# The first projection round in four stages of four row tiles, with groups of two blocks and transfers in a forced order

## The chip, the core and the metric

The kernel runs on one core of one Trainium2 chip. The metric is the device time in microseconds (us) of one execution. Before the change it is 1597.13 us, the median of 3 runs (1596.74 to 1597.31).

## The reference

One layer of a hybrid decoder over 256 tokens with 16 meta tokens ahead of them (272 columns), 2048 wide: a root-mean-square norm, one wide input projection, two mixing branches, an output projection, and a squared-ReLU MLP.

```
h = concat(meta_tokens, x)                       # 272 x 2048
xn = rmsnorm(h, norm_mix_g)
proj = xn @ w_in                                 # 2048 x 13336, split into q, k, v, gates
o_fox = forgetting_attention(...)                # 8 heads
o_gla = gated_linear_attention(...)              # 4 heads
y = sigmoid(gate_fox) * (o_fox @ w_o_fox) + sigmoid(gate_gla) * (o_gla @ w_o_gla)
h = h + y @ w_out
h = h + square(relu(rmsnorm(h, norm_mlp_g) @ w_ff1)) @ w_ff2
return rmsnorm(h, final_norm_g)[:, 16:]
```

The change touches only the first seven column blocks of `proj`, and how their operands reach the core.

## The kernel before, in words

Everything is kept transposed: features lie on the 128 partitions, tokens on the free axis, and the 2048 features are 16 row tiles (`KT`). Weights are cut on the host into blocks of 128 output columns; block c is `w_all[c]`, 128 rows of 16 x 128 values, 1 MB. A weight is split into a rounded part `whi` (a cast on ScalarE) and the rest `wlo` (a subtraction on VectorE), both in the type fp32r; an operand x likewise into `x_hi` and `x_lo`. For each row tile and block TensorE makes one wide product (`whi` by hi and lo tokens, 512 columns) and one narrow product (`wlo` by hi tokens, 256 columns); block 7 of the first round, which also needs the meta tokens, has three products of 272 columns instead.

Nearly all of the kernel works block after block: `weight_half` (L108) loads 8 row tiles of a block (512 KB), casts and subtracts, and `gemm2` or `gemm_all` runs the products. The very first round is different (L257 to L363). Since x itself arrives by row tiles, seven blocks (`NF`) run together, each in its own PSUM bank (L262), and the round goes through the row tiles. It has eight stages of two row tiles. In each, `load_h` (L286) fetches two row tiles of h (275 KB), and `load_stage` (L297) two weight pieces: blocks 1 to 4 (512 KB, `wa`) and blocks 5 to 7 (384 KB, `wb`). In stage 0 the first piece is loaded in two halves (L307, L308), blocks 1 and 2 ahead. Rows of a piece are runs of 1 KB.

The order of the work: for each row tile, ScalarE scales h by the norm's gain into `x_hi` (L324), VectorE makes `x_lo` (L325), GpSimd the meta columns of `x_lo` (L328, L329). Then `cut` casts a weight piece (L280) and subtracts (L281). The products of a stage come at L345 and L350, for block 7 at L347, L348 and L352. `square` (L289) squares four row tiles of h at once on ScalarE and adds them up on VectorE for the norm, after stages 3, 5, 6 and 7. The norm's factor is applied after the products, so nothing in the round waits for it. All loads are issued by SyncE.

Raw weights go through five buffers (`RAW`), hi and lo parts through five each (the pool `wp`), shared with all later blocks: a load waits until the piece five before it has been cast and subtracted, a cast until the products of the piece five before it have run. Stages 0 to 2 are loaded ahead, stage s + 3 at the start of stage s.

The framework plans the order on each engine by a model of its own (`schedule_with_timeline_sim`, L1054), so that an engine's order can differ from that of the program. `tc.issue_after(ins)` forces that what is written inside it comes behind `ins` on that engine. Before the change the planner is bound by it at few places: each h load of stages 3 to 7 behind a weight load, the squares behind a cast, and the constants (L369 to L372) behind the round's last load.

After the round: the seven banks are added up and released (L644 on), a small product for the gates' low-rank part runs (L654, L655), the norm's factor comes (L387), and the next block's product begins.

Of the kernel before, what the change touches and what calls it, by code (L numbers as in the profile page):

```python
# [7 lines left out]
F32 = mybir.dt.float32  # L8
# [3 lines left out]
AF = mybir.ActivationFunctionType  # L12
ALU = mybir.AluOpType
# [3 lines left out]
P = 128  # L17
D = 2048
KT = D // P
NM = 16  # L20
NT = 256
NA = NM + NT
# [9 lines left out]
RAW = 5  # L32
# [33 lines left out]
def trunk(ctx: ExitStack, tc: tile.TileContext, hT, w_small, w_all, consts, w_alpha2, out):  # L66
    nc = tc.nc
    serial = [0]

    def nm(s):  # L70
        serial[0] += 1
        return f"{s}_{serial[0]}"
# [11 lines left out]
    def bank(pool, s):  # L84
        return pool.tile([P, 512], F32, tag="bank", name=nm(s))
# [155 lines left out]
    def take(*shape):  # L241
        n = 1
        for d in shape:
            n *= d
        ap = room[:, at_room[0] : at_room[0] + n]
        at_room[0] += n
        if len(shape) == 2:
            ap = ap.rearrange("p (a b) -> p a b", b=shape[1])
        return ap
# [4 lines left out]
    def gain(i, k):  # L254
        return h[:, k, NA + i : NA + i + 1]
# [1 line left out]

    NF = 7  # L260
    warm = bank(px, "warm")
    first_ps = [bank(pg if c < 3 else px, "ps") for c in range(NF)]  # L262
    sqs = [take(4, NA) for _ in range(2)]
    acc = take(4, NA)
    meta = take(KT, NM)

    def first_weights(c0, n, k0):
        raw = wp.tile([P, HK * P], F32, tag="raw", name=nm("raw"), bufs=RAW)
        hi = wp.tile([P, HK, P], F32R, tag="whi", name=nm("whi"))
        lo = wp.tile([P, HK, P], F32R, tag="wlo", name=nm("wlo"))  # L270
        r, hi, lo = (t[:, 0 : 2 * n * P].rearrange("p (c k m) -> p c k m", k=2, m=P)
                     for t in (raw, hi.rearrange("p k m -> p (k m)"), lo.rearrange("p k m -> p (k m)")))

        def load(c, m):
            return nc.sync.dma_start(r[:, c : c + m], w_all[c0 + c : c0 + c + m, :, k0 * P : (k0 + 2) * P].rearrange(
                "c p (k m) -> p c k m", m=P))

        def cut(c, m, ks=slice(0, 2)):
            cs = slice(c, c + m)
            i = nc.scalar.copy(hi[:, cs, ks], r[:, cs, ks])  # L280
            nc.vector.tensor_tensor(lo[:, cs, ks], r[:, cs, ks], hi[:, cs, ks].bitcast(F32), op=ALU.subtract)  # L281
            return i.ins

        return hi, lo, load, cut

    def load_h(eng, k0, n):  # L286
        eng.dma_start(h[:, k0 : k0 + n, :], hT[:, k0 : k0 + n, :])

    def square(q):  # L289
        sq = acc if q == 0 else sqs[q % 2]  # L290
        nc.scalar.activation(sq, h[:, 4 * q : 4 * q + 4, 0:NA], AF.Square)
        if q:
            nc.vector.tensor_tensor(acc, acc, sq, op=ALU.add)

    stages = {}

    def load_stage(s, part):  # L297
        c0, n = ((0, 4), (4, 3))[part]
        w = first_weights(c0, n, 2 * s)
        stages.setdefault(s, []).append(w)  # L300
        return w[2](0, n) if s else w[2]

    load_a, load_b = load_stage(0, 0), load_stage(0, 1)
    load_h(nc.sync, 0, 2)
    load_a(0, 2)  # L307
    load_a(2, 2)  # L308
    load_b(0, 3)
    for cols in (NT, NT, NT, NT):  # L310
        nc.tensor.matmul(warm[:, 0:cols], ones[:, 0:P], ones[:, 0:cols], start=True, stop=True)
    for s in range(1, 3):
        load_h(nc.sync, 2 * s, 2)
        load_stage(s, 0)
        load_stage(s, 1)
    for s in range(KT // 2):
        if s + 3 < KT // 2:
            with tc.issue_after(load_stage(s + 3, 0).ins):
                load_h(nc.sync, 2 * s + 6, 2)
            last = load_stage(s + 3, 1).ins  # L320
        wa, wb = stages[s]
        for kk in range(2):
            k = 2 * s + kk
            nc.scalar.activation(x_hi[:, k], h[:, k, 0:NA], AF.Identity, scale=gain(0, k))  # L324
            nc.vector.scalar_tensor_tensor(x_lo[:, k, 0:NT], h[:, k, NM:NA], gain(0, k),  # L325
                                           x_hi[:, k, NM:].bitcast(F32), op0=ALU.mult, op1=ALU.subtract)
            xm = meta[:, k, :]
            nc.gpsimd.tensor_tensor(xm, h[:, k, 0:NM], gain(0, k).to_broadcast([P, NM]), op=ALU.mult)  # L328
            nc.gpsimd.tensor_tensor(x_lo[:, k, NT:], xm, x_hi[:, k, 0:NM].bitcast(F32), op=ALU.subtract)  # L329
            if s == 0:  # L330
                wa[3](0, 2, slice(kk, kk + 1))
            elif kk == 0:
                for w, n in ((wa, 4), (wb, 3)):
                    copied = w[3](0, n)
        if s == 0:
            wa[3](2, 2)
            for kk in range(2):
                copied = wb[3](0, 3, slice(kk, kk + 1))
        at = [(w[0][:, c], w[1][:, c]) for w, n in ((wa, 4), (wb, 3)) for c in range(n)]

        def products(c, k, part):
            hi, lo = at[c][0][:, k % 2, :], at[c][1][:, k % 2, :]
            ps, st, sp = first_ps[c], k == 0, k == KT - 1
            if part == 0 and c < NF - 1:
                nc.tensor.matmul(ps, hi, x[:, k], start=st, stop=False)  # L345
            elif part == 0:
                nc.tensor.matmul(ps[:, 0:NA], hi, x_hi[:, k], start=st, stop=False)  # L347
                nc.tensor.matmul(ps[:, X_LO], hi, x_lo[:, k], start=False, stop=sp, skip_group_check=True)  # L348
            elif c < NF - 1:
                nc.tensor.matmul(ps[:, 0:NT], lo, x[:, k, 0], start=False, stop=sp)  # L350
            else:
                nc.tensor.matmul(ps[:, 0:NA], lo, x_hi[:, k], start=False, stop=sp)  # L352

        if s < KT // 2 - 1:
            groups = [range(4), range(4, NF)] if s else [range(2), range(2, 4), range(4, NF)]
            order = [(c, 2 * s + kk, part) for g in groups for kk in range(2) for part in range(2) for c in g]
        else:
            order = [(c, 2 * s + kk, part) for c in range(NF) for kk in range(2) for part in range(2)]  # L360
        for o in order:
            products(*o)
        if s in (3, 5, 6, 7):  # L363
            with tc.issue_after(copied):
                square((3, 5, 6, 7).index(s))
    chunk[0] = NF
    nc.gpsimd.memset(wa2, 0.0)
    with tc.issue_after(last):
# [9 lines left out]
    for i in range(2):  # L378
        w = wp.tile([P, HK, P], F32R, tag="whi", name=nm("whi"))
# [269 lines left out]
    ps = bank(pg, "psa")  # L649
    for k in range(KT):  # L650
        if k == HK:
            norm1()
        w = small[k // HK][:, k % HK, :]
# [172 lines left out]
    for j0 in range(0, KT, 2):  # L826
        gates = ahead if j0 == 0 else [gate() for _ in range(4)]
        w = next_weights()
        for j in range(2):
            t = total(gemm2(w, of, k0=8 * j, nk=8))  # L830
            nc.vector.tensor_tensor(gates[2 * j], gates[2 * j], t, op=ALU.mult)
        for j in range(2):
            t = total(gemm2(next_weights(), og))
# [50 lines left out]
    acc = gat.tile([P, NT], F32, tag="acc", name="acc3", bufs=1)  # L884
    for g in range(NG):
        a = operand(keep, "a", tag="s1")
        held = []
        for f in range(KT):
            ps = gemm2(next_weights(), x2)
# [6 lines left out]
        last = g == NG - 1  # L896
# [98 lines left out]
    sqs = half(0, [none] * NL)  # L995
# [63 lines left out]
```

## Time and profile before

| | |
|---|---|
| median of 3 runs | 1597.13 us (1596.74 to 1597.31) |
| the profiled execution's own time | 1596.71 us |
| its span, from the first to the last instruction | 1595.0 us |
| TensorE busy | 1585.0 us, 99% |
| VectorE, ScalarE, GpSimd busy | 1060.4, 790.8, 125.2 us |
| mean rate of the transfers | 184 GB/s; 323 in the first fortieth of the span |

The profile shows one execution. Engines: PE is TensorE's matmul, PEld its weight load, DVE is VectorE, ACT is ScalarE, POOL is GpSimd, SP is SyncE, which issues transfers; a q behind a name (SPq) stands for an engine's instruction sequencer. Of a matmul the start is measured and the end modelled, so the time of one is read from start to start. In brackets stands how long the engine was idle before an instruction, and what released it. L345 is line 345 of the kernel before.

### The profile page before, as it was taken

To read this page: it belongs to the slowest core of one execution; us is meant where nothing else is said; L and a number is where in the kernel's file an instruction comes from. 1 tells how busy PE (TensorE), PEld (TensorE's weight loads), DVE (VectorE), ACT (ScalarE), POOL (GpSimd) and SP (SyncE) were. 2 spreads that over 40 slices of the span, in tenths; PEclk is the share of its full clock that TensorE was granted. 3 is DMA by queue.
4 is the path that set the end of the run, shared out by engine and by line. 5 is a ranking of instruction groups with operands and counts; after the bars stand their busy time and mean duration, and the time that the engine had idled before them with its cause. 6 is when DMAs were issued, how large, how long until landed. Compare 5 with 4: busy or idle time off the path is not lost.

```text
span 1595.0 us, 25427 instructions
## 1 busy us (share of the span) xinstructions
PE 1585.0 (99%) x9812; PEld 1428.8 (90%) x9812; DVE 1060.4 (66%) x1659; ACT 790.8 (50%) x1271; POOL 125.2 (8%) x213
## 2 busy tenths in 40 slices
PE   9999999999999999999999999999999999999997
PEld 8999999999998888888888888888888888888887
DVE  7897757676655555555777776567655776567655
ACT  6665444454455444444555544444444444444563
POOL 6011000011100000000011000000000000000022
PEclk9999999999999999999999999999999999999999
DMA  9444545454445555555555555555555555555552
GB/s 323 156 164 155 180 157 183 167 188 164 159 167 181 191 186 189 189 191 187 186 195 186 188 193 187 188 191 190 187 190 190 186 189 193 186 188 193 186 183 97
DMA packets 86602, 293.09 MB, mean 184 GB/s; under 512 B 9112, under 2 KB 16800, under 8 KB 86352
## 3 DMA queue, kind: packets, MB, share of 16 engines
q1 hardware_dynamic: 85872, 289.62, 53.8%
q8 instruction: 77, 1.26, 0.3%
q0 software_dynamic: 176, 1.12, 0.2%
q10 hardware_dynamic: 432, 0.72, 0.1%
q14 instruction: 45, 0.37, 0.1%
HBM read 289.32 MB, written 2.11 MB: 183 GB/s over the span
## 4 chain that ended last, share of the span: by engine, by line
PE 99%; DMA 0%; issue 0%; POOL 0%; ACT 0%; DVE 0%; SPq 0%; POOLq 0%; ACTq 0%
PE ps L136 51%; PE ps L137 27%; PE psa L155 5%; PE psa L154 5%; PE psa L153 5%; PE ps L345 1%; PE ps L350 1%; PE ps L928 1%; PE pa L548 1%; PE ps L912 0%; DMA raw<-w_all_dram 0%; PE po L611 0%; POOL o L976 0%; PE po L188 0%; PE ps L348 0%
## 5 line engine op out<-in xcount | busy, mean ns | idle before, releaser
L121 DVE TENSOR_TENSOR wlo<-raw,whi 128x1024 fp32r<-128x1024 f32 x522 | 641.0, 1228 | 452.8 <-ACT whi L120 449.4
L120 ACT CAST whi<-raw 128x1024 fp32r<-128x1024 f32 x522 | 548.1, 1050 | 660.0 <-PE ps L136 493.1
L136 PE MATMUL ps<-x,whi 128*128 128x512 f32 x1952 | 683.8, 393 | 0.0
L137 PE MATMUL ps<-x,wlo 128*128 128x256 f32 x1952 | 548.5, 281 | 0.0
L136 PEld LDWEIGHTS ps<-x,whi 128*128 128x128 f32 x1952 | 366.1, 188 | 80.4
L137 PEld LDWEIGHTS ps<-x,wlo 128*128 128x128 f32 x1952 | 368.3, 189 | 0.1
L136 PE MATMUL ps<-a,whi 128*128 128x512 f32 x960 | 334.3, 392 | 0.0
L137 PE MATMUL ps<-a,wlo 128*128 128x256 f32 x960 | 269.1, 281 | 0.0
L136 PEld LDWEIGHTS ps<-a,whi 128*128 128x128 f32 x960 | 179.8, 188 | 39.9
L137 PEld LDWEIGHTS ps<-a,wlo 128*128 128x128 f32 x960 | 181.1, 189 | 0.3
L153 PE MATMUL psa<-x,whi 128*128 128x272 f32 x624 | 181.2, 290 | 0.0
L155 PE MATMUL psa<-x,whi 128*128 128x272 f32 x624 | 181.1, 290 | 0.0
L154 PE MATMUL psa<-x,wlo 128*128 128x272 f32 x624 | 179.4, 288 | 0.0
L153 PEld LDWEIGHTS psa<-x,whi 128*128 128x128 f32 x624 | 118.1, 189 | 0.4
L154 PEld LDWEIGHTS psa<-x,wlo 128*128 128x128 f32 x624 | 117.4, 188 | 0.0
L155 PEld LDWEIGHTS psa<-x,whi 128*128 128x128 f32 x624 | 117.2, 188 | 0.0
L136 PE MATMUL ps<-og,whi 128*128 128x512 f32 x256 | 89.6, 392 | 0.0
L136 PE MATMUL ps<-y,whi 128*128 128x512 f32 x256 | 89.1, 392 | 0.0
L854 POOL TENSOR_TENSOR acc<-acc,hsq 128x256 f32<-128x256 f32 x26 | 28.5, 1097 | 769.2 <-ACT hsq L853 769.2
L137 PE MATMUL ps<-og,wlo 128*128 128x256 f32 x256 | 71.9, 281 | 0.0
L137 PE MATMUL ps<-y,wlo 128*128 128x256 f32 x256 | 71.8, 281 | 0.0
L171 DVE TENSOR_TENSOR evt<-ps,evb 128x256 f32<-128x256 f32 x158 | 65.9, 418 | 0.5 <-ACT evb L168 0.5
(301 smaller groups left out, 1437.0 us busy)
## 6 DMA issues: line engine op xcount, KB each, us to landing
raw<-w_all_dram SPq DMA_DIRECT2D x537, 512.0 KB, 3.6
raw<-w_all_dram SPq DMA_DIRECT2D x8, 384.0 KB, 6.6
h<-hT_dram SPq DMA_DIRECT2D x8, 275.0 KB, 6.7
negc<-fdram POOLq DMA_DIRECT2D x1, 1088.0 KB, 8.0
out_dram<-o SPq DMA_DIRECT2D x2, 512.0 KB, 2.7
raw<-w_all_dram SPq DMA_DIRECT2D x2, 256.0 KB, 3.9
room<-w_small_dram SPq DMA_DIRECT2D x1, 320.0 KB, 7.4
out_dram<-o ACTq DMA_DIRECT2D x1, 320.0 KB, 3.1
```

Of the source, the lines that this page charges most:

```text
L120: nc.scalar.copy(hi[:, k, :], r)
L121: nc.vector.tensor_tensor(lo[:, k, :], r, hi[:, k, :].bitcast(F32), op=ALU.subtract)
L136: nc.tensor.matmul(ps, hi, x, start=first, stop=False)
L137: nc.tensor.matmul(ps[:, 0:NT], lo, x[:, 0, :], start=False, stop=last)
L153: nc.tensor.matmul(ps[:, 0:NA], hi, x_hi[:, k], start=(k == 0), stop=False)
L154: nc.tensor.matmul(ps[:, 0:NA], lo, x_hi[:, k], start=False, stop=(k == KT - 1))
L155: nc.tensor.matmul(ps[:, X_LO], hi, x_lo[:, k], start=False, stop=(k == KT - 1), skip_group_check=True)
L171: nc.vector.tensor_tensor(t, ps[:, 0:NT], b, op=ALU.add)
L345: nc.tensor.matmul(ps, hi, x[:, k], start=st, stop=False)
L350: nc.tensor.matmul(ps[:, 0:NT], lo, x[:, k, 0], start=False, stop=sp)
L548: nc.tensor.matmul(dst, k[:, a], q[:, a, :], start=(a == 0), stop=(a == 1))
L854: nc.gpsimd.tensor_tensor(acc, acc, sq, op=ALU.add)
```

## The change

The round has four stages (`KS` = 4 row tiles each) of four groups: blocks 1 and 2, 3 and 4, 5 and 6, and 7 alone. Each pair of stage and group is a unit with one weight piece (512 KB, or 256 KB for block 7, in runs of 2 KB); there are 16, as there were 16 pieces. The first unit's piece is loaded block by block, and the first four row tiles of h two by two; later stages load four at once, ahead of their first unit. Each load is forced behind the one before it. Five units are loaded ahead, and unit i + 5 is loaded at unit i. The x tiles of a stage are made before its first unit is cut. The products of a group go row tile by row tile, in the last stage block by block. A stage's square comes after its second unit.

```diff
-    NF = 7
+    NF, KS = 7, 4
+    GROUPS = ((0, 2), (2, 2), (4, 2), (6, 1))
...
-    sqs = [take(4, NA) for _ in range(2)]
-    acc = take(4, NA)
+    sqs = [take(KS, NA) for _ in range(2)]
+    acc = take(KS, NA)
...
     def square(q):
         sq = acc if q == 0 else sqs[q % 2]
-        nc.scalar.activation(sq, h[:, 4 * q : 4 * q + 4, 0:NA], AF.Square)
+        nc.scalar.activation(sq, h[:, KS * q : KS * q + KS, 0:NA], AF.Square)
...
-    def load_stage(s, part):
-        c0, n = ((0, 4), (4, 3))[part]
-        w = first_weights(c0, n, 2 * s)
-        stages.setdefault(s, []).append(w)
-        return w[2](0, n) if s else w[2]
...
-    load_a, load_b = load_stage(0, 0), load_stage(0, 1)
-    load_h(nc.sync, 0, 2)
-    load_a(0, 2)
-    load_a(2, 2)
-    load_b(0, 3)
...
+    units = [(s, c0, n) for s in range(KT // KS) for c0, n in GROUPS]
+    loaded, queue = [], [None]
+
+    def in_turn(load, *args):
+        with tc.issue_after(queue[0]) if queue[0] else nullcontext():
+            queue[0] = load(*args).ins
+
+    def load_unit():
+        i = len(loaded)
+        s, c0, n = units[i]
+        w = first_weights(c0, n, KS * s)
+        loaded.append(w)
+        if i == 0:
+            in_turn(load_h, nc.sync, 0, 2)
+            in_turn(w[2], 0, 1)
+            in_turn(w[2], 1, 1)
+            in_turn(load_h, nc.sync, 2, 2)
+        else:
+            if c0 == 0:
+                in_turn(load_h, nc.sync, KS * s, KS)
+            in_turn(w[2], 0, n)
...
-        if s < KT // 2 - 1:
-            groups = [range(4), range(4, NF)] if s else [range(2), range(2, 4), range(4, NF)]
-            order = [(c, 2 * s + kk, part) for g in groups for kk in range(2) for part in range(2) for c in g]
-        else:
-            order = [(c, 2 * s + kk, part) for c in range(NF) for kk in range(2) for part in range(2)]
+    for _ in range(RAW):
+        load_unit()
+    for i, (s, c0, n) in enumerate(units):
+        w = loaded[i]
+        cs = range(c0, c0 + n)
+        if i == 0:
+
+            for k in range(KS):
+                x_tile(k)
+                if k % 2:
+                    for c in cs:
+                        copied = w[3](c, 1, slice(k - 1, k + 1))
+            order = [(c, k + kk, part) for k in (0, 2) for c in cs for kk in range(2) for part in range(2)]
+        else:
+            if c0 == 0:
+                for k in range(KS * s, KS * s + KS):
+                    x_tile(k)
+            copied = w[3](0, n)
+            if s < KT // KS - 1:
+                order = [(c, KS * s + kk, part) for kk in range(KS) for part in range(2) for c in cs]
             else:
-                nc.tensor.matmul(ps[:, 0:NA], lo, x_hi[:, k], start=False, stop=sp)
...
+                order = [(c, KS * s + kk, part) for c in cs for kk in range(KS) for part in range(2)]
+        if len(loaded) < len(units):
+            load_unit()
         for o in order:
-            products(*o)
-        if s in (3, 5, 6, 7):
+            products(w, c0, *o)
+        if c0 == 2:
             with tc.issue_after(copied):
-                square((3, 5, 6, 7).index(s))
+                square(s)
+    last = queue[0]
```

`first_weights` takes `KS` row tiles per piece instead of 2. `x_tile` and `products` hold the same instructions as before, as functions. The constants are loaded behind the last unit's load.

## Rows read from the trace of the kernel before

**Rows 1.** The page's first section: busy us (share of the span) and instructions by engine.
```profile
PE 1585.0 (99%) x9812; PEld 1428.8 (90%) x9812; DVE 1060.4 (66%) x1659; ACT 790.8 (50%) x1271; POOL 125.2 (8%) x213
```

**Rows 2.** All waits of TensorE: us in total, times, longest.
```profile
PE warm L311 <- DVE ones L195: 1.3, 1, 1.3
PE pn L952 <- ACT sq L933: 0.7, 1, 0.7
PE ps L345 <- ACT whi L280: 0.4, 1, 0.4
```

**Rows 3.** TensorE's timeline, end of the round: start us, us, what.
```profile
40.74 0.39 PE L345 MATMUL ps<-x,whi 128*128 128x512 f32 x1
...
44.91 0.29 PE L347 MATMUL ps<-x,whi 128*128 128x272 f32 x1
...
45.29 0.29 PE L347 MATMUL ps<-x,whi 128*128 128x272 f32 x1
...
45.67 0.29 PE L207 MATMUL prb<-csh,ones 128*128 128x272 f32 x1
...
49.93 0.28 PE L153 MATMUL psa<-x,whi 128*128 128x272 f32 x1
```

**Rows 4.** Timeline of all engines, 0 to 12 us.
```profile
4.55 0.70 ACT L280 CAST whi<-raw 128x256 fp32r<-128x256 f32 x2
...
5.00 0.96 PE L345 MATMUL ps<-x,whi 128*128 128x512 f32 x2
5.08 0.81 DVE L281 TENSOR_TENSOR wlo<-raw,whi 128x256 fp32r<-128x256 f32 x2
...
6.40 0.62 ACT L280 CAST whi<-raw 128x512 fp32r<-128x512 f32 x1 [1.15 <-DMA raw<-w_all_dram]
...
7.51 0.93 ACT L280 CAST whi<-raw 128x384 fp32r<-128x384 f32 x2 [0.49 <-DMA raw<-w_all_dram]
...
8.27 0.90 POOL L328 TENSOR_TENSOR room<-h 128x16 f32<-128x16 f32 x2 [2.65 <-DMA h<-hT_dram]
8.34 0.93 ACT L324 ACTIVATE x<-h 128x272 fp32r<-128x272 f32 x2
...
9.70 1.89 ACT L280 CAST whi<-raw 128x1024 fp32r<-128x1024 f32 x2 [0.43 <-DMA raw<-w_all_dram]
...
11.00 1.54 PE L345 MATMUL ps<-x,whi 128*128 128x512 f32 x6
```

**Rows 5.** TensorE's timeline in short windows: the first products, and the pause.
```profile
5.56 0.40 PE L345 MATMUL ps<-x,whi 128*128 128x512 f32 x1
...
6.26 0.40 PE L345 MATMUL ps<-x,whi 128*128 128x512 f32 x1
...
7.07 0.50 PE L345 MATMUL ps<-x,whi 128*128 128x512 f32 x1 [0.41 <-ACT whi L280]
...
7.40 0.39 PE L345 MATMUL ps<-x,whi 128*128 128x512 f32 x1
7.63 0.54 PE L350 MATMUL ps<-x,wlo 128*128 128x256 f32 x3
```

**Rows 6.** The round as one stretch: us, PE, PEld, DVE, ACT, POOL busy, PEclk, DMA, GB/s.
```profile
5.00:45.67 40.67, 40.26 (x241) 35.72 (x241) 31.61 (x47) 29.15 (x46) 20.87 (x34) 1.00 0.94 310
```

**Rows 7.** Casts and subtractions of 1024 columns in the round: busy us, mean ns.
```profile
L281 DVE TENSOR_TENSOR wlo<-raw,whi 128x1024 fp32r<-128x1024 f32 x7 | 8.6, 1225 | 3.5 <-ACT whi L280 3.5
...
L280 ACT CAST whi<-raw 128x1024 fp32r<-128x1024 f32 x7 | 7.3, 1041 | 2.3 <-DMA raw<-w_all_dram 2.3
```

**Rows 8.** ScalarE's timeline: the first square, and the next block's first cast.
```profile
18.43 1.11 ACT L291 ACTIVATE room<-h 128x1088 f32<-128x1088 f32 x1
...
40.83 1.05 ACT L120 CAST whi<-raw 128x1024 fp32r<-128x1024 f32 x1
```

**Rows 9.** Two stretches early in the round, columns as in rows 6.
```profile
4.00:6.00 2.00, 2.00 (x7) 1.22 (x6) 1.63 (x4) 1.25 (x4) 1.59 (x5) 1.00 0.78 216
7.00:10.00 3.00, 2.93 (x18) 2.66 (x19) 2.53 (x5) 2.08 (x6) 1.71 (x4) 1.00 1.07 373
```

More of the change, by code (lines that the diff above doesn't have):

```diff
@@ L270, in first_weights, with cut @@
         lo = wp.tile([P, HK, P], F32R, tag="wlo", name=nm("wlo"))
-        r, hi, lo = (t[:, 0 : 2 * n * P].rearrange("p (c k m) -> p c k m", k=2, m=P)
+        r, hi, lo = (t[:, 0 : KS * n * P].rearrange("p (c k m) -> p c k m", k=KS, m=P)
                      for t in (raw, hi.rearrange("p k m -> p (k m)"), lo.rearrange("p k m -> p (k m)")))
         def load(c, m):
-            return nc.sync.dma_start(r[:, c : c + m], w_all[c0 + c : c0 + c + m, :, k0 * P : (k0 + 2) * P].rearrange(
+            return nc.sync.dma_start(r[:, c : c + m], w_all[c0 + c : c0 + c + m, :, k0 * P : (k0 + KS) * P].rearrange(
                 "c p (k m) -> p c k m", m=P))
-        def cut(c, m, ks=slice(0, 2)):
+        def cut(c, m, ks=slice(0, KS)):
             cs = slice(c, c + m)
@@ L286, in load_h @@
     def load_h(eng, k0, n):
-        eng.dma_start(h[:, k0 : k0 + n, :], hT[:, k0 : k0 + n, :])
+        return eng.dma_start(h[:, k0 : k0 + n, :], hT[:, k0 : k0 + n, :])
     def square(q):
         sq = acc if q == 0 else sqs[q % 2]
-        nc.scalar.activation(sq, h[:, 4 * q : 4 * q + 4, 0:NA], AF.Square)
+        nc.scalar.activation(sq, h[:, KS * q : KS * q + KS, 0:NA], AF.Square)
         if q:
             nc.vector.tensor_tensor(acc, acc, sq, op=ALU.add)
-    stages = {}
-    def load_stage(s, part):
-        c0, n = ((0, 4), (4, 3))[part]
-        w = first_weights(c0, n, 2 * s)
-        stages.setdefault(s, []).append(w)
-        return w[2](0, n) if s else w[2]
@@ L305, in trunk, with x_tile @@
-    load_a, load_b = load_stage(0, 0), load_stage(0, 1)
-    load_h(nc.sync, 0, 2)
-    load_a(0, 2)
-    load_a(2, 2)
-    load_b(0, 3)
+    def x_tile(k):
+        nc.scalar.activation(x_hi[:, k], h[:, k, 0:NA], AF.Identity, scale=gain(0, k))
+        nc.vector.scalar_tensor_tensor(x_lo[:, k, 0:NT], h[:, k, NM:NA], gain(0, k),
+                                       x_hi[:, k, NM:].bitcast(F32), op0=ALU.mult, op1=ALU.subtract)
+        xm = meta[:, k, :]
+        nc.gpsimd.tensor_tensor(xm, h[:, k, 0:NM], gain(0, k).to_broadcast([P, NM]), op=ALU.mult)
+        nc.gpsimd.tensor_tensor(x_lo[:, k, NT:], xm, x_hi[:, k, 0:NM].bitcast(F32), op=ALU.subtract)
@@ new lines, in products @@
+    def products(w, c0, c, k, part):
+        hi, lo = w[0][:, c - c0, k % KS, :], w[1][:, c - c0, k % KS, :]
+        ps, st, sp = first_ps[c], k == 0, k == KT - 1
+        if part == 0 and c < NF - 1:
+            nc.tensor.matmul(ps, hi, x[:, k], start=st, stop=False)
+        elif part == 0:
+            nc.tensor.matmul(ps[:, 0:NA], hi, x_hi[:, k], start=st, stop=False)
+            nc.tensor.matmul(ps[:, X_LO], hi, x_lo[:, k], start=False, stop=sp, skip_group_check=True)
+        elif c < NF - 1:
+            nc.tensor.matmul(ps[:, 0:NT], lo, x[:, k, 0], start=False, stop=sp)
+        else:
+            nc.tensor.matmul(ps[:, 0:NA], lo, x_hi[:, k], start=False, stop=sp)
@@ L310, in trunk @@
     for cols in (NT, NT, NT, NT):
         nc.tensor.matmul(warm[:, 0:cols], ones[:, 0:P], ones[:, 0:cols], start=True, stop=True)
[L312 to L350, printed above, removed]
-            else:
-                nc.tensor.matmul(ps[:, 0:NA], lo, x_hi[:, k], start=False, stop=sp)
-        if s < KT // 2 - 1:
-            groups = [range(4), range(4, NF)] if s else [range(2), range(2, 4), range(4, NF)]
-            order = [(c, 2 * s + kk, part) for g in groups for kk in range(2) for part in range(2) for c in g]
-        else:
-            order = [(c, 2 * s + kk, part) for c in range(NF) for kk in range(2) for part in range(2)]
@@ new lines, in trunk @@
+    for _ in range(RAW):
[10 more added lines that the diff above has]
+            order = [(c, k + kk, part) for k in (0, 2) for c in cs for kk in range(2) for part in range(2)]
+        else:
+            if c0 == 0:
[4 more added lines that the diff above has]
+                order = [(c, KS * s + kk, part) for kk in range(KS) for part in range(2) for c in cs]
+            else:
+                order = [(c, KS * s + kk, part) for c in cs for kk in range(KS) for part in range(2)]
+        if len(loaded) < len(units):
+            load_unit()
```

## The prediction, made before the change was run

> **What bounds the kernel now.** I read the page's totals first, then TensorE's waits, and only then the first 46 us, where the whole change lies. TensorE is busy for 1585.0 us, 99% of the span [rows 1], and the only waits that it has anywhere are 1.3 us for the ones at the start, 0.7 us at the end and 0.4 us for a cast in the first round [rows 2]. So a transfer, a cast or a subtraction costs time only where TensorE stands for it, and in the first round that can be counted.
>
> Work of the round: with the operands there, twelve pairs of a wide and a narrow product run from 40.74 to 44.91, 0.347 us each, and the three products of block 7 take 0.38 us (44.91 to 45.29) [rows 3]. One row tile is thus 6 x 0.347 + 0.38 = 2.46 us, and 16 of them 39.4 us. The round takes from 5.00 [rows 4] to 45.67 [rows 3], 40.67 us. **1.3 us are lost in it now**: about 0.3 us on the very first product, which took 0.56 us (5.00 to 5.56) instead of 0.23 (7.40 to 7.63), about 0.6 us between the starts at 6.26 and 7.07 [rows 4, 5] (0.23 us would do; the idle time in that row is only 0.41 because it counts from a modelled end), and some 0.4 us in small pieces. From 7.07 on TensorE is full: 40.26 us busy in the 40.67 [rows 6].
>
> So no more than 1.3 us can be won in the round, 0.08% of 1597 us. What a measurement of this kernel can tell from no change is about 0.2%, 3.2 us.
>
> **The change, part by part.** The 240 products, their weight loads and all bytes stay. Seventeen weight transfers stay seventeen; eight of h become five, so SyncE issues 22 instead of 25. Casts become 4 of 256 columns, 11 of 1024 and 4 of 512 instead of 19 of other sizes, over the same columns. These edits cost nothing by themselves, since ScalarE and VectorE work 29.15 and 31.61 of the 40.67 us [rows 6] beside TensorE; without that cover a lengthened cast would cost its full length. What counts is when each operand is there.
>
> Start. The first product needs 275 KB of h, then 256 KB of weights, as now, and comes at 5.00 again, behind one cast of 256 columns [rows 4].
>
> Block 2. Now the next 256 KB carry blocks 3 and 4; after the change they carry block 2, which the first products have without them today. They land at 6.40, where the waiting cast starts. One 256-column cast is 0.35 us (two take 0.70) [rows 4], so block 2 starts at about 6.8. Block 1 has two row tiles by then, 0.69 us of work and the same slow first product, and is done at about 6.05. **Idle 0.75 us.** Block 2's narrow products wait for VectorE's subtraction, 0.4 us (two take 0.81 [rows 4]), half of it hidden; its two row tiles end at 7.7. The bound on the other side, an earlier landing, is rival one.
>
> Row tiles 3 and 4. 275 KB of h took 0.76 us in the queue (7.51 to 8.27 [rows 4]); from 6.4 this makes 7.2. An x tile is 0.47 us on ScalarE (two take 0.93 [rows 4]) and a pass of about 0.4 on VectorE, and in program order the casts for these rows stand behind both x tiles: TensorE goes on at 8.1 (if the planner puts the casts first, their weights having landed) to 8.45. **Idle 0.4 to 0.75 us.** Four pairs, 1.39 us, end at 9.5 to 9.85.
>
> Blocks 3 and 4. 512 KB took 1.43 us (8.27 to 9.70 [rows 4]), so they land at 8.6. One cast of 1024 columns is 1.04 us and its subtraction 1.23 [rows 7]: with ScalarE free at 8.75, the wide products can start at 9.8, the narrow ones at 11.0. If the planner puts all eight wide products first (it does such things: the six wide ones in a row at 11.00 [rows 4] are out of the written order), only 0.3 us is lost; in written order 0.5 us is. **Idle 0.1 to 0.7 us.**
>
> These pieces with the slow first product: 0.33 + 0.75 + 0.2 + 0.4 to 0.75 + 0.1 to 0.7, 1.8 to 2.7 us lost, against 0.9 us in the same stretch now.
>
> Later blocks. Each transfer of 512 KB takes 1.43 us and feeds eight pairs, 2.78 us of TensorE. Blocks 5 and 6 land at 10.0 and block 7 at 10.8, before TensorE asks for them at 12.5 to 13.4. The first square, 1.11 us on ScalarE, now at 18.43 [rows 8], may come between these casts, as it is tied only to the cast of blocks 3 and 4: 0 to 0.4 us. Stage two: h of four row tiles lands at 12.3, weights at 13.7; four x tiles take 1.9 us, cast and subtraction 2.3, so ready at 16.5, with TensorE busy to 16.8 or 17.7. It holds, but narrowly.
>
> SyncE's forced order. A load waits for the raw buffer of five units before, and all later ones, h too, queue behind it. What hides this is five units of look-ahead, five times 2.5 us of TensorE; a load late by more than that would cost the rest. Zero.
>
> End of the round. The next block's first cast waits for a hi buffer of this round: now at 40.83 [rows 8], used at 49.93 [rows 3]. The last stage goes block by block in longer pieces, so that buffer comes free 1 to 2 us later, and the slack is several us: zero. Banks are evicted earlier: zero, as nothing waits for them.
>
> **Sum.** 0.9 to 1.8 us more lost in stage one, 0 to 0.4 for the square, small gaps as now: +0.9 to +2.2 us. I take +1.2, nearer the lower end, because of the planner's reordering in the row just named. The profiled execution is 1596.71 us around a span of 1595.0, and 0.42 below the median; +1.2 makes 1597.9 of it, and of the median of 1597.13 **1598.3 us**. Bounds: -1.3 (all present loss gone) to +2.2.
>
> **A rule against it.** The row first: after its present pause TensorE goes on with 0.33 and then 0.23 us for a wide product [rows 5], at a granted clock of 1.00 before and behind it [rows 9]. The Trainium skill, TensorE: Matmul & The Clock Gate, section Part 1: The HAM clock gate, says that the array's default is half its clock, and that idling gives the full clock back. By that rule the pauses that the change adds could drop it to the lower level, and the time would be that of rival three.
>
> **Rivals.**
> One, the early transfers come faster and the pauses shrink. Between 4 and 6 us only 216 GB/s flowed, between 7 and 10 us 373 [rows 9]; at the later pace the second 256 KB take 0.7 us and would land at 5.2 instead of 6.40, since the first landed before the cast at 4.55 [rows 4]. For it: the runs are 2 KB instead of 1 KB. Against: nothing in the profile says that the run's length made the slow stretch. Then block 2 follows block 1 at once, h comes at 6.0, and the loss is 0.9 to 1.8 us instead of 1.3: -0.4 to +0.5, **1597.2 us**. Chance 24%.
>
> Two, slower by more than 0.2%: the early pace lasts, and stage two starves. At 216 GB/s from 7.2 on, blocks 3 and 4 land at 9.6, 5 and 6 at 12.1, 7 at 13.3, the 550 KB of h at 15.9 and the next weights at 18.3; ready at 20.6 while TensorE ends stage one at 18.3. That is 2.3 us, and 0.9 for the later start, beyond the forecast: **1601.5 us**. It decides from where stage two's first weights land after about 15.5. Against: in that very place the trace has 373 GB/s. Chance 5%.
>
> Three, the clock falls in the pauses. The 4.9 us of work between 7 and 13 us would take 4.9 us more at the 1.2 GHz level than at 2.4: up to **1603 us**. Against: the row above, and pauses of 0.75 us at most. Chance 3%.
>
> Four, the change moves nothing that TensorE sees: the planner fills the pauses with other products, and it stays full from 7 us on: 1597.1 us. Chance 8%.
>
> **Numbers.** Forecast 58%; 24, 5, 3 and 8% for one to four; 2% for what I don't see. The range takes in the lower bound of -1.3 (1595.8) and goes past the upper one of +2.2 (1599.3) by 1.1 us, for a landing of block 2 or of blocks 3 and 4 that late again: 1595.8 to 1600.4. Slower by over 0.2% are two, three and nothing of the forecast's own bounds: 8%. Faster by over 0.2% would need 3.2 us where 1.3 are to be had: 2%. The rest, 90%, is within 0.2%.
>
> **What would show it.** Right: first product at 5.0, a pause of some 0.7 us before block 2 ended by a cast, another before row tile 3 ended by x or a cast, the round's end at 46.5 to 48.0 instead of 45.67, and the same shape from there on. Wrong: a round that ends at 45.2 or before, waits of TensorE after 18 us, a granted clock below 1.00 inside the round, or a difference that arises behind it.

## The result, and the profile after

The kernel after takes **1599.73 us** (median of 22 runs, 1598.89 to 1601.23); beside it, on the same chips, the one before takes 1596.93 us (22 runs, 1596.6 to 1598.25). The ratio is 1.0017, 95% interval 1.0011 to 1.0023: slower by 2.8 us, just inside the 0.2% that count as no change here. The forecast of 1598.3 had the sign; the size is above it, and inside the range. One execution of the second experiment below (1941.52 us), one of the fourth (1721.81) and a few of the kernel before beside them were far longer than the rest; they are left out of the ratios and of what is said on the clock.

The profiled execution of the kernel after took 1599.13 us, 2.4 more than that of the kernel before. First the page's totals, columns as in [rows 1]:

```profile
span 1597.4 us, 25421 instructions
...
PE 1586.0 (99%) x9812; PEld 1428.9 (89%) x9812; DVE 1061.5 (66%) x1659; ACT 791.4 (50%) x1271; POOL 123.2 (8%) x213
```

All engines do nearly what they did [rows 1]; the span is 2.4 us longer. What TensorE waited for, in the view of its waits, columns as in [rows 2]:

```profile
PE warm L341 <- DVE ones L195: 1.3, 1, 1.3
PE ps L331 <- ACT whi L281: 0.9, 2, 0.5
PE pn L958 <- ACT sq L939: 0.7, 1, 0.7
PE ps L336 <- DVE wlo L282: 0.5, 1, 0.5
PE ps L331 <- DVE x L298: 0.2, 1, 0.2
```

The first and the third line were there before. The 0.4 us for a cast [rows 2] have become 0.9 us for two casts, and a subtraction (`wlo`) and an x tile are new. Where they lie is seen in the timeline of all engines, 0 to 13 us (columns as in [rows 4]):

```profile
3.86 0.94 ACT L297 ACTIVATE x<-h 128x272 fp32r<-128x272 f32 x2 [1.77 <-DMA h<-hT_dram]
...
4.96 0.71 ACT L281 CAST whi<-raw 128x256 fp32r<-128x256 f32 x2 [0.16 <-DMA raw<-w_all_dram]
...
5.42 0.80 PE L331 MATMUL ps<-x,whi 128*128 128x512 f32 x1 [0.36 <-ACT whi L281]
...
6.01 0.45 PE L336 MATMUL ps<-x,wlo 128*128 128x256 f32 x1
...
6.25 0.50 PE L331 MATMUL ps<-x,whi 128*128 128x512 f32 x1
...
6.59 0.28 PE L336 MATMUL ps<-x,wlo 128*128 128x256 f32 x1
6.92 0.71 ACT L281 CAST whi<-raw 128x256 fp32r<-128x256 f32 x2 [1.25 <-DMA raw<-w_all_dram]
...
7.37 0.50 PE L331 MATMUL ps<-x,whi 128*128 128x512 f32 x1 [0.50 <-ACT whi L281]
...
8.74 0.50 PE L331 MATMUL ps<-x,whi 128*128 128x512 f32 x1 [0.17 <-DVE x L298]
...
8.98 1.05 ACT L281 CAST whi<-raw 128x1024 fp32r<-128x1024 f32 x1 [0.41 <-DMA raw<-w_all_dram]
...
9.94 1.10 ACT L292 ACTIVATE room<-h 128x1088 f32<-128x1088 f32 x1
10.07 1.23 DVE L282 TENSOR_TENSOR wlo<-raw,whi 128x1024 fp32r<-128x1024 f32 x1 [0.97 <-ACT whi L281]
...
10.24 0.63 PE L331 MATMUL ps<-x,whi 128*128 128x512 f32 x2
...
11.35 0.51 PE L336 MATMUL ps<-x,wlo 128*128 128x256 f32 x2 [0.48 <-DVE wlo L282]
...
13.10 0.63 PE L331 MATMUL ps<-x,whi 128*128 128x512 f32 x2
```

Read it from start to start, at 0.23 us for a wide and 0.12 us for a narrow product. The first product comes at 5.42 instead of 5.00 [rows 4]: its cast stood for the transfer until 4.96. Block 1's four products take 1.29 us (5.42 to 6.71, 0.12 behind the start at 6.59) for 0.69 us of work: **0.6 us lost**. Then TensorE stands until 7.37 for block 2's cast, which stood 1.25 us for its transfer: **0.66**. Between 7.37 and 8.74 lie 1.37 us for 0.69 of work again, **0.68** (some 0.2 of it for block 2's subtraction, the rest before and at row tile 3). At 10.24 two wide products start, end at 10.70, and the narrow ones behind them wait for the subtraction of 1024 columns to 11.35: **0.65**. The next unit follows at 13.10 with no wait. The end of the round, in TensorE's timeline:

```profile
47.69 0.28 PE L338 MATMUL ps<-x,wlo 128*128 128x272 f32 x1
47.81 0.29 PE L660 MATMUL psa<-x,whi 128*128 128x272 f32 x1
...
52.08 0.29 PE L153 MATMUL psa<-x,whi 128*128 128x272 f32 x1
```

The round ends at 47.81 instead of 45.67 [rows 3], 2.14 us later, and the product at L153 comes at 52.08 instead of 49.93 [rows 3]: the same 2.15. It stays so to the last product, which starts at 1589.19 instead of 1587.04. The remaining 0.25 us of the span lie behind that, at the last stores. The round as one stretch, columns as in [rows 6]:

```profile
5.42:47.81 42.39, 41.24 (x240) 35.85 (x241) 32.26 (x48) 29.92 (x47) 17.75 (x34) 1.00 0.84 291
```

Of 42.39 us some 3.0 are lost, against 1.27 before: 1.72 more, and 0.42 for the later start. Hardly anything is lost or won after 12 us.

### The profile page after: what moved, and what is told of

Same layout as the page of the kernel before. It is cut to its first block, busy times and chain, and to the rows that moved or that the text cites. A ratio compares the mean times of both kernels' runs of the same rounds, so it can differ in the third digit from the quotient of the medians.

```text
span 1597.4 us, 25421 instructions
## 1 busy us (share of the span) xinstructions
PE 1586.0 (99%) x9812; PEld 1428.9 (89%) x9812; DVE 1061.5 (66%) x1659; ACT 791.4 (50%) x1271; POOL 123.2 (8%) x213
## 4 chain that ended last, share of the span: by engine, by line
PE 98%; DMA 0%; issue 0%; POOL 0%; DVE 0%; ACT 0%; SPq 0%; POOLq 0%; ACTq 0%
PE ps L136 51%; PE ps L137 27%; PE psa L155 5%; PE psa L154 5%; PE psa L153 5%; PE ps L331 1%; PE ps L336 1%; PE ps L934 1%; PE pa L554 1%; PE ps L918 0%; DMA raw<-w_all_dram 0%; PE po L617 0%; POOL o L982 0%; PE po L188 0%; PE psa L661 0%
## 5 line engine op out<-in xcount | busy, mean ns | idle before, releaser
L153 PE MATMUL psa<-x,whi 128*128 128x272 f32 x624 | 181.2, 290 | 0.0
L153 PEld LDWEIGHTS psa<-x,whi 128*128 128x128 f32 x624 | 118.1, 189 | 0.4
```

The costliest lines, as they stand in the source:

```text
L153: nc.tensor.matmul(ps[:, 0:NA], hi, x_hi[:, k], start=(k == 0), stop=False)
```

## The experiments

Theory A: the loss is work that is not there. With two blocks at a time, the first pieces that land carry half the TensorE work per x tile, so TensorE outruns the transfers, and nothing else matters. Rivals: B, the forced order of the transfers costs it; C, the landing of the first weights is later for their shape (runs of 2 KB); D, the pauses bring TensorE to its lower level. The experiments are counted in the order of their headings; the last is the second of the two kernels under the last heading.

### The forced order taken away

```diff
-        with tc.issue_after(queue[0]) if queue[0] else nullcontext():
-            queue[0] = load(*args).ins
+        queue[0] = load(*args).ins
```

> The changed kernel without the forced order of its loads; the planner then issues the h loads of the second, third and fourth stage earlier, from the ninth load on. Theory A (the whole loss is TensorE waiting for operands in the first 12 us, because two blocks at a time give it half the work per landed x tile): no change, ratio to before 1.0012 to 1.0022, round's end at 47.8 us +-0.3. Rival B (the forced order queues loads behind waits): 1 us or more comes back, ratio under 1.001.

Measured: 1600.16 us (11 runs), ratio 1.0019 (1.0011 to 1.0028), that of the kernel after. Without the force the h loads of the third and fourth stage are issued at 6.32 and 7.87 us instead of 13.66 and 20.59, and nothing comes back of the 1 us or more that B wanted: the forced order costs nothing, and **B falls**. The profiled execution was a long one (1601.14 us), with the round's end at 49.75, which no theory had. TensorE's timeline tells why:

```profile
8.33 0.80 PE L330 MATMUL ps<-x,whi 128*128 128x512 f32 x1 [0.68 <-ACT whi L281]
...
9.17 0.63 PE L330 MATMUL ps<-x,whi 128*128 128x512 f32 x1
...
9.60 0.41 PE L335 MATMUL ps<-x,wlo 128*128 128x256 f32 x1
...
49.75 0.29 PE L659 MATMUL psa<-x,whi 128*128 128x272 f32 x1
```

The wide product at 9.17 takes 0.43 us to the next start, twice 0.23, and so it goes until 13.5 us. In that execution the first weights had landed at 5.49 (4.93 in the kernel after) and block 2's at 7.85 (6.89). The windows of that execution (columns as in [rows 9]) show it from another side:

```profile
9.10:12.40 3.30, 3.30 (x13) 2.75 (x12) 2.13 (x4) 2.88 (x4) 0.95 (x3) 1.00 1.04 412
```

Thirteen products in 3.3 us, TensorE "busy" throughout, where full pace gives nineteen; the granted clock is printed as 1.00 all the same, since the trace's first record of the clock stands only at 13.5 us.

### The first four row tiles as before, the other twelve as after

The round begins with two stages of two row tiles and groups of four and three blocks; from row tile 5 on it has the stages, groups and forced order of the change.

```diff
-    units = [(s, c0, n) for s in range(KT // KS) for c0, n in GROUPS]
+    units = [(k0, 2, c0, n) for k0 in (0, 2) for c0, n in ((0, 4), (4, 3))]
+    units += [(k0, KS, c0, n) for k0 in range(KS, KT, KS) for c0, n in GROUPS]
...
```

> The first four row tiles go as before the change (two stages of two, blocks 1 to 4 and 5 to 7, runs of 1 KB), the other twelve as after it, all loads forced. Theory A: first product at 5.0, one pause of about 0.6 us, round's end at 45.7 us +-0.4, ratio 0.9995 to 1.0005. Rival B: the loss stays, ratio above 1.001. If the rest of the new scheme (groups of two, runs of 2 KB, longer last stage) were worth anything, the round would end before 45.4.

Measured: 1597.32 us (11 runs), ratio 1.0003 (0.9994 to 1.0011). The timeline:

```profile
4.56 0.70 ACT L281 CAST whi<-raw 128x256 fp32r<-128x256 f32 x2
...
5.00 0.73 PE L330 MATMUL ps<-x,whi 128*128 128x512 f32 x2
...
5.81 0.62 ACT L281 CAST whi<-raw 128x512 fp32r<-128x512 f32 x1 [0.56 <-DMA raw<-w_all_dram]
...
45.58 0.29 PE L663 MATMUL psa<-x,whi 128*128 128x272 f32 x1
```

First product at 5.00, end of the round at 45.58 (before 45.67 [rows 3]). Within the interval, **all of the loss comes from the first four row tiles**; the other three quarters of the change, and the forced order once more, cost and bring nothing that shows.

### The first piece by rows: blocks 1 and 2 together, two row tiles of them at a time

```diff
...
-            in_turn(w[2], 0, 1)
-            in_turn(w[2], 1, 1)
+            in_turn(w[2], 0, 2, 0, 2)
             in_turn(load_h, nc.sync, 2, 2)
+            in_turn(w[2], 0, 2, 2, 4)
```

> The changed kernel, but its first weight piece is loaded as rows 1 and 2 of both blocks (runs of 1 KB), then h of row tiles 3 and 4, then rows 3 and 4 of both blocks. Theory A: block 2 follows block 1 without a pause, but the pause before row tile 3 grows, as the same bytes must have landed by then: TensorE goes on there at 8.4 to 8.7 (8.74 after the change), gain 0 to 0.4 us. Rival C (runs of 2 KB made the first landings late by 0.5 us): first weights land at 4.4 instead of 4.9, first product at 5.0, and all that follows comes 0.5 us earlier: gain 0.5 to 0.8 us.

Measured: 1599.15 us (11 runs), ratio 1.0015 (1.0006 to 1.0023). In TensorE's timeline:

```profile
7.71 0.81 PE L331 MATMUL ps<-x,whi 128*128 128x512 f32 x2 [0.95 <-ACT whi L281]
...
47.86 0.29 PE L660 MATMUL psa<-x,whi 128*128 128x272 f32 x1
```

The first product came at 4.95, as C had it, the pause before block 2 was gone, and TensorE was at row tile 3 a whole microsecond earlier (7.71, not 8.74; A had 8.4 to 8.7). In the profiled execution the round ended where it had (47.86): the time was lost again, in three waits for casts and one for a subtraction, because blocks 3 and 4 land no sooner. **A pause moved is not a pause won**, and C's earlier first landing by itself is worth nothing in that execution. The median is 0.6 us below that of the kernel after, which is a gain of the size that C wanted, but the two intervals overlap, and the profile shows no such gain. One of these eleven runs has a mean clock of 0.997, against nine of the 22 of the kernel after; whether that is the difference stays open.

### The pauses filled

The warm-up is half a product longer, and behind block 1's four products five more run into the warm-up's bank, which nothing reads.

```diff
-    for cols in (NT, NT, NT, NT):
+    for cols in (NT, NT, NT, NT, P):
...
+                    for _ in range(5):
+                        with tc.issue_after(mm.ins):
+                            mm = nc.tensor.matmul(warm[:, 0:NT], ones_r[:, 0:P], ones_r[:, 0:NT], start=True, stop=True)
```

> The changed kernel with TensorE kept busy in its first two pauses: one more warm-up product of 128 columns ahead of the first product, and five products of the ones (0.12 us each) between block 1 and block 2, into a bank that nobody reads. Theory A (waiting for operands alone): the same time to +0.2 us, and the same spread between executions. Rival D (part of the loss is TensorE at its lower clock level because of the pauses, in some executions more than in others): the clock is granted in full about 1 us earlier than at 6.46, the mean granted clock of all executions is 0.998 or more, the slower half of the executions disappears, and the median falls by 0.4 to 0.9 us.

Measured: 1599.53 us (12 runs), ratio 1.0017 (1.0008 to 1.0026). TensorE's timeline:

```profile
6.85 0.76 PE L372 MATMUL warm<-ones 128*128 128x256 f32 x5
...
47.58 0.29 PE L673 MATMUL psa<-x,whi 128*128 128x272 f32 x1
```

The round ends 0.23 us sooner, as much as blocks 3 and 4 landed sooner (their cast began at 8.76, not 8.98), and the median falls by 0.2, of the 0.4 to 0.9 that D wanted. Nor did full pace begin earlier, as D had it: the narrow product at 6.29 still took 0.22 us to the next start. The mean granted clock was 0.998 or 0.999 in its runs, where 9 of the 22 of the kernel after have 0.997. So **D is at most a small part** of the median.

### The kernel before, its first stage row tile by row tile

The way opposite to the change: more blocks per x tile, in pieces of one row tile (runs of 512 bytes).

```diff
...
-    load_h(nc.sync, 0, 2)
-    load_a(0, 2)
-    load_a(2, 2)
-    load_b(0, 3)
+    prev = load_h(nc.sync, 0, 1)
+    for ld, args in ((load_a, (0, 2, 0, 1)), (load_a, (2, 2, 0, 1)), (load_h, (nc.sync, 1, 1)),
+                     (load_b, (0, 3, 0, 1)), (load_a, (0, 4, 1, 2)), (load_b, (0, 3, 1, 2))):
...
```

> The kernel before, whose first stage goes row tile by row tile over all seven blocks: h of row tile 1 alone (137 KB), then its weights for blocks 1 and 2, 3 and 4, then h of row tile 2, then the rest (runs of 512 B). Theory A (the start is bound by the bytes that must have landed per us of TensorE's work): 265 KB instead of 531 KB stand before the first product, so it comes 0.3 to 0.8 us earlier than 5.0, and the round ends 0 to 0.8 us before 45.67, at most 0.05% of the time. Rival C (short runs land late): the first weights land no earlier than 4.3, and the round ends at 45.7 or later.

Measured: 1598.09 us (11 runs), ratio 1.0008 (1.0000 to 1.0017). TensorE's timeline:

```profile
4.50 1.35 PE L347 MATMUL ps<-x,whi 128*128 128x512 f32 x4
...
7.11 0.73 PE L347 MATMUL ps<-x,whi 128*128 128x512 f32 x2 [0.79 <-ACT whi L280]
...
46.94 0.29 PE L207 MATMUL prb<-csh,ones 128*128 128x272 f32 x1
```

The start came half a microsecond earlier, as A had it, but the gain was lost and 1.3 us besides: a pause of 0.79 at 7.11 and another of 0.98 at 12.1, since the pieces of the second stage landed at 11.03 instead of 9.68. Against A in its plain form: work per x tile is not all, the arrival of the following pieces counts as much. The first weights (128 KB) were cast from 3.59 on, so short runs did not make them late, as C had it.

### The first block in two halves, in runs of 1 KB

```diff
...
-            in_turn(w[2], 0, 1)
+            in_turn(w[2], 0, 1, 0, 2)
+            in_turn(w[2], 0, 1, 2, 4)
```

> The changed kernel, but its very first weight load (block 1, four row tiles, 256 KB in runs of 2 KB) goes as two loads of 128 KB in runs of 1 KB. If the length of the runs made the first landing late (4.9 to 5.5 us where two blocks in runs of 1 KB landed at 4.3), both halves have landed by 4.4 and the first product comes at 5.0. If it is that one block is read at a time, or anything else, the second half lands at 4.9 or later; the first half, half the bytes, may land before 4.5 either way. The time stays within 0.1% of the changed kernel's in both.

Measured: 1601.72 us (9 runs), ratio 1.0028 (1.0018 to 1.0037). The timeline:

```profile
4.38 0.39 ACT L281 CAST whi<-raw 128x256 fp32r<-128x256 f32 x1
...
5.28 0.40 ACT L281 CAST whi<-raw 128x256 fp32r<-128x256 f32 x1 [0.52 <-DMA raw<-w_all_dram]
...
7.72 0.51 PE L332 MATMUL ps<-x,whi 128*128 128x512 f32 x1 [1.07 <-ACT whi L281]
```

The whole 256 KB of block 1 are there at 5.26, later than in runs of 2 KB (4.93), so C's "2 KB" alone is not the reason. Block 2 starts at 7.72 (7.37 after), and the time grew where no theory had it grow. Its profiled execution (1599.48 us) has a mean clock of 0.999; the other eight have 0.996 or 0.997, and take 1600.18 to 1602.49.

### The kernel before with half of the warm-up

```diff
-    for cols in (NT, NT, NT, NT):
+    for cols in (NT, NT):
```

> The kernel before with two warm-up products instead of four, so that TensorE stands idle from 3.3 to 5.0 us; nothing else changes. Rival D (idle time ahead of the first product holds TensorE at its lower level for longer, and that was part of what the change cost): wide products take 0.43 instead of 0.23 us for 3 us and more after 5.0, the round ends 0.7 to 2 us after 45.67, ratio 1.0004 to 1.0013. Theory A alone: round's end within 0.3 us of 45.67.

Measured: 1597.94 us (11 runs), ratio 1.0006 (0.9997 to 1.0015). TensorE's timeline:

```profile
6.78 1.91 PE L345 MATMUL ps<-x,whi 128*128 128x512 f32 x4
...
47.75 0.29 PE L207 MATMUL prb<-csh,ones 128*128 128x272 f32 x1
```

Here products went at half pace (0.43 us for a wide one, 0.21 for a narrow one) until 11.2 us, and the profiled round ended at 47.75, 2.08 late, of which 0.3 is a later first landing. So **D's mechanism exists**: in this execution TensorE ran at its lower level for some microseconds, with less work ahead of the first product. That less work is what brings it is made likely, not shown, since one execution of the first experiment did the same behind the whole warm-up. The median grew by only 1.0 us, so most executions paid less than the profiled one, which was the longest of its kernel.

### Blocks 3 and 4 cut in two halves

To take the wait at 11.35 away, the cast and the subtraction of 1024 columns go as two of 512.

```diff
-            copied = w[3](0, n)
+            if i == 1:
+                w[3](0, n, slice(0, 2))
+                copied = w[3](0, n, slice(2, 4))
+            else:
+                copied = w[3](0, n)
```

> The changed kernel, but the piece of blocks 3 and 4 in its first stage is cast and subtracted in two halves, row tiles 1 and 2, then 3 and 4. Theory A: the wait of 0.48 us for the subtraction at 11.35 goes, and the products after it come 0.5 to 0.9 us earlier; round's end 0.5 to 0.9 us earlier than it would be at the same landing of the piece (47.81 at a landing of 8.96). If TensorE's pace there were set by something else, the wait stays.

Measured: 1600.09 us (10 runs), ratio 1.0019 (1.0009 to 1.0028). TensorE's waits:

```profile
PE ps L331 <- ACT whi L281: 2.5, 2, 1.9
```

The wait for the subtraction is gone, yet nothing is gained: in the profiled execution the first weights landed at 5.20 and block 2's at 8.27, a pause of 1.88 us. Behind it the windows show the clock fall (columns as in [rows 9]):

```profile
9.10:12.40 3.30, 3.30 (x11) 2.71 (x11) 2.59 (x6) 2.88 (x5) 1.45 (x4) 0.50 1.04 410
12.50:15.00 2.50, 2.50 (x15) 2.17 (x15) 1.50 (x2) 2.50 (x6) 1.20 (x2) 1.00 1.04 381
```

A granted clock of 0.50 (1.2 GHz) and 11 products in 3.3 us, then 1.00 (2.4 GHz) again. What the halved cut is worth by itself stays open, since the landing and the clock covered it.

### What the landing hangs on: two kernels

The first 256 KB of weights landed 0.65 to 0.68 us behind h in the four kernels that load them as two blocks of two row tiles at once (before, the second, the third and the seventh experiment), and 1.09 to 1.85 us behind it where they are one block of four row tiles (after, and the first, fourth and eighth experiment). Two kernels part block and run length: the kernel before with its first piece block by block (1 KB runs), and the kernel after with its first two blocks in one transfer (2 KB runs).

```diff
-    load_a(0, 2)
-    load_a(2, 2)
+    for c in range(4):
+        load_a(c, 1)
```

> The kernel before, whose first 512 KB of weights (blocks 1 to 4, two row tiles) go as four loads of one block each instead of two loads of two blocks; runs of 1 KB as before. From the landing of the first h to that of these 512 KB it took 2.1 to 2.7 us where blocks were read in pairs, 3.0 to 4.8 us in the changed kernel, which reads them one at a time. If reading one block at a time is what makes the landings late: 3.0 us or more here, round's end 0.3 us or more behind 45.67, ratio 1.0002 to 1.001. If it is the run's length or the number of row tiles: 2.1 to 2.7 us, round's end as before.

```diff
-            in_turn(w[2], 0, 1)
-            in_turn(w[2], 1, 1)
+            in_turn(w[2], 0, 2)
```

> The changed kernel, but its first weight piece (blocks 1 and 2, four row tiles, 512 KB, runs of 2 KB) is one load instead of two of one block. If reading one block at a time makes the landings late: the 512 KB land 2.1 to 2.7 us behind the first h, at 5.8 to 6.5 instead of 6.9 to 8.3; the first product comes later (6.2 to 6.9 instead of 5.4), but everything from row tile 3 on comes 0.5 us or more earlier than in the changed kernel, except for what the lower clock level costs after the longer idle time. If it is the length of the runs: 3.0 us or more again, and the time is that of the changed kernel or longer.

Measured: 1597.38 us (10 runs), ratio 1.0002 (0.9992 to 1.0011), and 1599.48 us (11 runs), ratio 1.0017 (1.0008 to 1.0026). The timeline of the first:

```profile
5.05 0.71 ACT L280 CAST whi<-raw 128x256 fp32r<-128x256 f32 x2 [0.41 <-DMA raw<-w_all_dram]
...
6.25 0.62 ACT L280 CAST whi<-raw 128x512 fp32r<-128x512 f32 x1 [0.48 <-DMA raw<-w_all_dram]
```

and of the second:

```profile
6.32 1.33 ACT L281 CAST whi<-raw 128x256 fp32r<-128x256 f32 x4 [1.74 <-DMA raw<-w_all_dram]
...
47.66 0.29 PE L659 MATMUL psa<-x,whi 128*128 128x272 f32 x1
```

The first 512 KB landed 2.49 and 2.68 us behind h, as in the kernel before (2.69), against 3.05 in the kernel after: neither single blocks nor 2 KB runs make that late alone, and what does **stays open**. The traces say where to look. When the first 256 KB of weights had landed, the queues had moved 0.69 to 0.76 MB in the four early kernels and 0.70 to 0.78 MB in the four late ones, so the bytes were about the same. The pace was not: between 3.5 and 5.0 us it was 219 to 264 GB/s in the early four, and 230, 194, 156 and 112 GB/s in the late four, in the order of their lateness. What slows it, no run shows.

Two things can be read besides. With single blocks the first 256 KB came 1.28 us behind h, and the round of the kernel before ends 0.8 us later (46.46; 0.4 in the median, within the noise), but not for that: block 7's last product of row tile 2 starts at 10.73, 0.14 us sooner than before, and only then TensorE waits for the casts of the second stage, whose pieces landed at 10.32 and 11.69 instead of 9.68 and 10.74. And the last kernel starts 1.4 us later than the kernel after (6.78, not 5.42) and still ends its round at 47.66: what sets the end there is when blocks 3 and 4 can run, not when block 1 does.

## Why the prediction was right, and where it was off

**The place and the kind** were right. The whole loss lies before 12 us, the shape behind it is the same, 2.15 us later, and none of the late waits came. The pauses are those foretold: before block 2 for a cast (0.66 us, foretold 0.75), block 2's narrow products (0.23; 0.2), row tile 3 for an x tile (0.45; 0.4 to 0.75). The sign that failed is the first product, at 5.42 and not at 5.0. The zeros held: the square came at 9.94 to 11.04 between two casts and TensorE did not wait for it, stage two starved nothing, the forced order cost nothing (first and second experiment), nor did the end of the round.

**The size was off by a factor of about two**: +1.2 foretold, +2.15 at the end of the round, +2.4 in the profiled execution, +2.8 between the medians. The sum's own bounds, +0.9 to +2.2, just hold the round's +2.15; the median is inside the range only by the 1.1 us that the range allowed beyond them for a late landing. Three terms:

- "Start: comes at 5.00 again" is 0.42 us short. I read the landing of 256 KB from [rows 4] as if a transfer's bytes alone set it. As two blocks of two row tiles they came 0.66 us behind h, as one block of four 1.09. The same lateness is in block 2, landed at 6.89 instead of 6.40; there it cost nothing more in the pause, as the pause began later too.
- The first products: 0.6 us lost, foretold 0.33. The narrow product at 6.01 still took 0.24 us to the next start, half pace, and the second wide one 0.34 us. The prediction took the slow first product as a fixed price. It is the clock: the trace's first record of the full clock stands at 5.50 us before and at 6.46 us after, and the 1.00 that [rows 9] prints for 4 to 6 us does not tell it.
- "I take +1.2, nearer the lower end, because of the planner's reordering" was the wrong choice: blocks 3 and 4 ran in the written order, two wide products and then two narrow ones, and lost 0.65 us, near the upper end of the foretold 0.1 to 0.7. That the planner had once put six wide products in a row [rows 4] was no evidence for this place.

With the pieces as measured, 0.60 + 0.66 + 0.23 + 0.45 + 0.65, the stretch lost 2.59 us from the first product on, at the upper end of the 1.8 to 2.7 foretold. Against the 0.9 of before that is +1.7, and with 0.42 for the start 2.1.

**That sum says where the time lies, not what each term costs.** In five kernels with the groups of the change, the round ends 38.82 or 38.83 us behind the start of the cast of blocks 3 and 4, wherever between 4.82 and 6.78 us the first product came. From ScalarE's timelines of the third, fourth, sixth and last experiment, in this order, and TensorE's of the sixth:

```profile
9.04 1.05 ACT L281 CAST whi<-raw 128x1024 fp32r<-128x1024 f32 x1 [1.07 <-DMA raw<-w_all_dram]
...
8.76 1.05 ACT L281 CAST whi<-raw 128x1024 fp32r<-128x1024 f32 x1 [0.39 <-DMA raw<-w_all_dram]
...
9.46 1.05 ACT L281 CAST whi<-raw 128x1024 fp32r<-128x1024 f32 x1 [0.60 <-DMA raw<-w_all_dram]
48.28 0.29 PE L661 MATMUL psa<-x,whi 128*128 128x272 f32 x1
...
8.83 1.05 ACT L281 CAST whi<-raw 128x1024 fp32r<-128x1024 f32 x1 [0.34 <-DMA raw<-w_all_dram]
```

| kernel | first product | cast of blocks 3 and 4 | end of the round | from cast to end |
|---|---|---|---|---|
| after | 5.42 | 8.98 | 47.81 | 38.83 |
| third experiment | 4.95 | 9.04 | 47.86 | 38.82 |
| fourth | 5.70 | 8.76 | 47.58 | 38.82 |
| sixth | 4.82 | 9.46 | 48.28 | 38.82 |
| last | 6.78 | 8.83 | 47.66 | 38.83 |

Each of these casts waited for its transfer, and behind it TensorE waits for the subtraction (at 11.35 in the kernel after). Whatever is lost ahead of that wait only makes it shorter. So in these executions the late start, the slow first products and the first pauses cost nothing by themselves, and what was mis-sized is the landing of blocks 3 and 4, foretold at 8.6, together with the choice of the planner's order behind it. An estimate from these rows: landed at 8.6, the written order would end the round near 47.45, +1.8, the upper end of what the sum had for stage one; the landing 0.36 us later makes the +2.14. (In the first and the eighth experiment, at half pace behind that cast, it is 39.82 and 39.14.)

**The rivals.** One (early transfers faster) did not come: 215 GB/s flowed between 4 and 6 us, as before, and block 2 landed later, not sooner. Two (stage two starves) and four (nothing moves) did not come. Three, the clock, is the one that I put too low at 3%. In the profiled execution of the kernel after, the clock is at its full level from 6.46 us to the end of the round, but by mean clock its 22 runs part: 1599.32 us on average at 0.999 (7 runs), 1599.68 at 0.998 (6), 1600.24 at 0.997 (9). Without these nine the median is 1599.29, 2.4 us above the kernel before, as the profiled execution is. In the eighth experiment an execution shows the fall itself, behind a pause of 1.88 us, and it costs there some 1.7 us (half of the stretch between 9.1 and 12.4), not the 4.9 of the rival; a pause of 1.72 us in the last experiment brought none. That a part of the 0.4 us between medians and profiled executions is this has been argued, not shown: filling the pauses gave back 0.2.

Beside the row of 0.50: the Trainium skill, TensorE: Matmul & The Clock Gate, section Part 1: The HAM clock gate, says that half clock is the default and that activity releases the throttle (the prediction's "gives the full clock back" means that idling loses it); the seventh experiment agrees (two warm-up products fewer, half pace until 11.2 us), and so does the eighth.

## What to carry to other kernels

In a kernel that is bound by TensorE from its first microseconds on, as this one is, a change of this kind can move only the start, and there transfers are best ordered by the TensorE work that a landed kilobyte releases: many blocks for few row tiles first, fewer and longer pieces later. The fifth experiment shows the limit: in still smaller pieces the first product came sooner, and the round ended 1.27 us later, since the pieces behind it came later. The same bytes landed at different times here, between shapes and within one shape, so an operand's arrival is to be bounded, not carried over. And a pause taken away is worth nothing until the operand that ends the next one comes sooner.

## What was not expected of the hardware

- The first 256 KB of weights landed between 0.65 and 1.85 us behind the same h, depending on how they were cut, and within one cut too: 1.09, 1.55, 1.69 and 1.85 us in four kernels that issue it alike. This is the least certain quantity of the whole case.
- TensorE's lower level lasted to 11.2 us in the seventh and 13.5 us in the first experiment, while TensorE was busy. The granted clock is printed as 1.00 for such a stretch at the start of an execution, though products run at half pace, because the trace has no record of the clock before the first rise; there the distance between starts tells the level.
- A mean clock of 0.997 or 0.996 goes with longer times: 9 of the 22 runs of the kernel after, and eight of nine with the first block halved, which lie 0.7 to 3.0 us over its profiled one. The kernel before and its variants have none, not even the one that begins with the smallest pieces. In the eighth experiment the one fall takes 0.001 off the mean; that the others are such falls is argued from it. A mean of 0.998 against 0.999 says little: it counts the stretch at 0.50 behind the last product that every trace has, and not a start at half pace, and in the kernel before the two groups differ by 0.2 us at most.
